# One transformer layer on one core: the first feed-forward chunk half by block products, the late modulation in 1024-wide steps, five held weight tiles at the output product's tail

## The chip, the core and the metric

The kernel runs on one core of a Trainium2 chip. A core has the matrix engine (PE, with its weight load PEld), the vector engine (DVE), the scalar engine (ACT), GpSimd (POOL) and the sync engine (SP), which here only issues DMA transfers; 16 DMA engines move the data of all queues. The metric is the device time of one execution in microseconds (us); smaller is better.

## The reference

One layer of a diffusion backbone for 128 context tokens and 512 latent tokens (640 rows, 1024 features), in float32. With SiLU(cond) through one matrix come six modulation vectors for each of the two token groups:

```python
sh1, sc1, g1, sh2, sc2, g2 = modulation(c, w_mod, b_mod)
h = rmsnorm(x, n1) * (1 + sc1) + sh1
aq, ak, av, bq, bk, bv, ga, gb = split(h @ w_in)
a_o = attention(aq, ak, av)                    # grouped-query, rotary on latents
b_o = neighbourhood_attention(bq, bk, bv)      # 8 x 16 window, learned bias
m = sigmoid(ga) * (a_o @ w_br_a) + sigmoid(gb) * (b_o @ w_br_b)
x = x + g1 * (m @ w_out)
h2 = rmsnorm(x, n2) * (1 + sc2) + sh2
x = x + g2 * (square(relu(h2 @ w_mlp_in)) @ w_mlp_out)    # 1024 -> 4096 -> 1024
y = rmsnorm(x, final_norm_g)
```

Outputs are y for both groups and the new keys and values of the context tokens.

## The kernel before

**Numbers in two parts.** Every product is done in float32 precision by splitting both operands into a high and a low part of the matrix engine's rounded type: `w_hi*x_hi + w_hi*x_lo + w_lo*x_hi`, three matmuls for each 128x128 weight block and each half of the 640 tokens (`HALVES`, 320 columns). So each weight tile that arrives by DMA is converted: ACT copies the high part, and the low part is made by DVE, by POOL, or (keys in `LOACC`) by ACT writing the negated high part and a DMA of POOL's queue adding the weights from memory onto it.

**Stages.** Features lie on partitions, tokens on columns. After the input projection and attention (which end at about 313 us) come four stages that matter here:

1. *The merge* (the loop that fills `M`, about 313 to 449 us). For each of eight feature tiles n: gate products from `w_in` tiles 18+n and 26+n (two halves each, 24 matmuls a unit, followed by `sigmoid` on ACT), then four branch products of 12 matmuls, whose PSUM results DVE multiplies with the gates (L1190), adds (L1191) and splits (ACT L1192, DVE L1193). For n = 3 and 4 both gates were computed earlier and are read back from memory by POOL's queue. `Units.ps` hands out seven PSUM banks in rotation, so unit u+7 can start once unit u has been read.
2. *The output product* (449 to 506 us). `order(KT, 4)`: the first four tiles with both halves, then the first halves of the last four, then their second halves. Four weight tiles are held for that tail: three in the ordinary pool, one in `EXTRA`. `add_gated` adds the result to x; `sq_add` accumulates the squares; `rstd_half` makes the norm of a half with two matmuls on a matrix of ones.
3. *The first feed-forward chunk* (506 to 564 us): 1024 of the 4096 hidden features, eight `w1` tiles, each a plain product with both halves. In the same stretch DVE and ACT form the second norm (`norm2`, `modulate`) and the combinations of it (`t_pieces`: T1 to T4) that later chunks need.
4. *The pairs* (564 to 922 us): `SEQ`. Layer 1 of chunks 1 to 3 and layer 2 of all chunks go by pairs of output tiles with a seven-product scheme (Strassen-Winograd): a pair takes 7 block products (A11, A12, S1 to S4, A22) of 12 matmuls where the plain way takes 8 (96 matmuls). `Operands` loads the weight tiles, adds blocks of them by accumulating DMAs of POOL's queue, and converts them ahead; six weight tiles at most are live (`W.live`).

**Late modulation.** `late_mods` computes the four modulation vectors that are needed from the output product on, as dot products on DVE. 32 tiles of 128x1024 (`wmt`, 512 KB) come by SP's queue into three buffers (tag `ms`); each takes four DVE instructions of 512 columns (L1111: two halves times two groups). A *step* is two of them. `mod_pace` spreads the 64 steps over merge and output product: every PSUM unit earns credit, and each step costs `MCOST`.

**Order.** In the merge and the output product DVE executes in the order of the program text (`MAN`); the other engines' order, and DVE's from the first chunk on, comes from the framework's scheduler. SP issues its transfers in order; a transfer whose buffer is not free holds up those behind it.

Of the kernel before, what the change touches and what calls it, by code (L numbers as in the profile page):

```python
# [16 lines left out]
P = 128  # L17
# [11 lines left out]
WP1 = 0  # L29
# [9 lines left out]
MCOST = 1500  # L39
DEFER = 60  # L40
LAG = (0, 4)
# [16 lines left out]
BLKPOOL = (("A12", "A22"), ())  # L58
# [4 lines left out]
LOTAIL = tuple(("S4", n) for n in range(4))  # L63
# [5 lines left out]
LOACC = (("in", 21, 22), ("in", 29, 30), ("in", 20, 23), ("in", 25, 26), ("in", 28, 34), ("br", 0, 8))  # L69
# [5 lines left out]
def trunk_layer(ctx: ExitStack, tc: tile.TileContext, xT, small_in, wmodA, wmodB, tabs, cacheK, cacheV, bias,  # L75
# [43 lines left out]

    def tt_tile(name):  # L120
        return cur["p"].tile([P, NT], F32R, tag="tt", bufs=12, name=name)
# [77 lines left out]
    def sq_add(acc, x, f, sl):  # L199

        q = acc if f == 0 else u("sq")
        ACT.activation(q[:, sl], x[:, sl], AF.Square)
        if 0 < f < KT - 1:
            DVE.tensor_add(acc[:, sl], acc[:, sl], q[:, sl])
        return q

    def rstd_half(acc, last, rstd, sl):
        p, n = ps_t(), sl.stop - sl.start
        PE.matmul(p[:, :n], ones, acc[:, sl], start=True, stop=False)
        PE.matmul(p[:, :n], ones, last[:, sl], start=False, stop=True)  # L210
        ACT.activation(rstd[:, sl], p[:, :n], AF.Ln, bias=eps)
        ACT.activation(rstd[:, sl], rstd[:, sl], AF.Exp, scale=-0.5)


    def w_order():
# [10 lines left out]
        for n in range(KT):  # L226
            yield ("w1", n), w1[n]
# [12 lines left out]
    class Weights:  # L240
        def __init__(self):
            self.order = list(w_order())
            self.pos = {k: i for i, (k, _) in enumerate(self.order)}
            self.st, self.t = {}, {}
            self.nd = self.nc = self.live = self.busy = 0
            self.extra = self.defer = False
# [9 lines left out]
        def conv(self):  # L256
# [4 lines left out]
            if key in EXTRA:  # L261
                self.extra = True
                hi, lo = (dp.tile([P, KT, P], F32R, tag="w4" + x, bufs=1, name="w4") for x in "hl")
# [24 lines left out]
        def done(self, *key):  # L288

            if key in EXTRA:  # L290
                self.extra = False
# [4 lines left out]
        def ahead(self):  # L296
            while self.nc < len(self.order):
                key = self.order[self.nc][0]
                if key in EXTRA and self.extra:
                    return  # L300
# [7 lines left out]
    WPOOLSET = {("out", n) for n in range(WPO, KT)} | {("w1", n) for n in range(WP1)}  # L308
    EXTRA = {("out", 4), ("w1", 0)}
# [788 lines left out]
    def late_mods():  # L1098

        cb = [tt_tile("cb") for _ in range(4)]  # L1100
        for i in range(2):
            for q in range(2):
                MISC.dma_start(r32(cb[2 * q + i][:, :512]),
                               silu[i, 4 * q:4 * q + 4].rearrange("k p -> (k p)").partition_broadcast(P))
        for n in MODS:
            st = dp.tile([P, 1024], F32, tag="ms", bufs=3, name="wmt")
            DQ[QM].dma_start(st, wmodB[n])
            for q in range(2):
                for i in range(2):
                    t = dp.tile([P, 512], F32, tag="mt", bufs=2, name="mt")  # L1110
                    DVE.scalar_tensor_tensor(t, st[:, q * 512:(q + 1) * 512], 1.0, r32(cb[2 * q + i][:, :512]), op0=OP.mult,  # L1111
                                             op1=OP.mult, accum_out=parts[:, q, n, i:i + 1])
                if q == 0:
# [122 lines left out]
    def norm_pieces(acc, last, rstd, h, apply):  # L1236
        return [lambda: None] * LAG[h] + [lambda: rstd_half(acc, last, rstd, HALVES[h])] + [lambda f=f: apply(range(f, min(f + NG, KT)))
                                                     for f in range(0, KT, NG)]

    def norm2(fs, h):  # L1240
        mod_step(16 + 4 * (fs.stop + -fs.stop % MG) - lm_n[0])
        modulate([(H2[f], X1[f], mod(2, f), mod(1, f)) for f in fs], rstd2, h)

    X1 = {}
    acc2, rstd2 = u("acc2"), u("rstd2")
    H2 = [h_pair(f"hh{f}") for f in range(KT)]
    Wt = {}
    for n, h in order(KT, 4):
        if n not in Wt:
            Wt[n] = W.get("out", n)  # L1250
            X1[n] = o_tile(f"x1_{n}")
            nc.sync.dma_start(X1[n], xT[:, n, :])
        ps = unit(Wt[n], M, h)
        if h:
            W.done("out", n)
        add_gated(n, ps, h, 0)
        sq = sq_add(acc2, X1[n], n, HALVES[h])
        if n < KT - 4 or h == 0 and n < KT - 1:
            mod_pace(OU)
        elif n == KT - 1:  # L1260
            side += norm_pieces(acc2, sq, rstd2, h, lambda fs, h=h: norm2(fs, h))

    def final(fs, sl):
        for f in fs:
            DVE.tensor_mul(X1[f][:, sl], X1[f][:, sl], rstd3[:, sl])
            (nc.sync, nc.scalar)[f % 2].dma_start(yT[:, f, sl], X1[f][:, sl])

    def relu2(dst, src, h):  # L1270

        r, sl = u("rl"), HALVES[h]
        ACT.activation(r[:, :HT], src, AF.Relu)
        if RL:
            ACT.activation(r[:, :HT], r[:, :HT], AF.Square)
            ACT.activation(dst[0][:, sl], r[:, :HT], AF.Copy)
        else:
            ACT.activation(dst[0][:, sl], r[:, :HT], AF.Square)

        def rest():  # L1280
            if not RL:
                DVE.tensor_mul(r[:, :HT], r[:, :HT], r[:, :HT])
            DVE.tensor_sub(dst[1][:, sl], r[:, :HT], r32(dst[0][:, sl]))
        flush_later(posts)
        posts.append(rest)


    T = [{}, {}, {}]
    L0, L1 = slice(0, HT), slice(HT, NT)

    def t_pieces(k):
        raw = {}

        def cut(dst, src, sl0, sl1):
            ACT.activation(dst[0][:, sl0], src, AF.Copy)
            later.append(lambda: DVE.tensor_sub(dst[1][:, sl1], src, r32(dst[0][:, sl0])))

        def p0():
            if k == 2:
                mod_step(64 - lm_n[0])  # L1300
            for i in range(3):
                T[i][k] = tt_tile(f"t{i + 1}_{k}")
            for i in range(2):
                raw[i] = u("hr")
                DVE.tensor_add(raw[i], r32(H2[k + 4 * i][0]), r32(H2[k + 4 * i][1]))
            raw[2] = u("t12")
            DVE.tensor_sub(raw[2][:, L0], raw[0][:, L1], raw[0][:, L0])
            cut((T[0][k], T[0][k]), raw[2][:, L0], L0, L1)

        def p1():  # L1310
            DVE.tensor_sub(raw[2][:, L1], raw[1][:, L1], raw[2][:, L0])
            cut((T[1][k], T[1][k]), raw[2][:, L1], L0, L1)

        def p2():
            DVE.tensor_sub(raw[0][:, L0], raw[1][:, L1], raw[0][:, L1])
            cut((T[2][k], T[2][k]), raw[0][:, L0], L0, L1)

        def p2b():
            t4[k] = tp2.get()
            DVE.tensor_sub(t4[k], raw[1][:, L0], raw[2][:, L1])  # L1320

        def p3():
            cut(H2[k], t4[k], L1, L1)
            for t in H2[k + 4]:
                ACT.activation(t[:, L1], r32(t[:, L1]), AF.Copy, scale=-1.0)

        return [p0, p1, p2, p2b, p3]
# [4 lines left out]
    def formed(i):  # L1332
# [8 lines left out]
    FIRST0 = [("A11", 0), ("A11", 1), ("A11", 2), ("A12", 0), ("A12", 1), ("A11", 3), ("A12", 2), ("A12", 3)]  # L1341
    FIRST2 = [("A11", 0), ("S1", 3, 1), ("A11", 1), ("S4", 3, 1), ("A12", 0), ("A12", 1),
              ("A11", 2), ("A11", 3), ("A12", 2), ("A12", 3)]

    def products():

        for c in range(4):
            for o, n in FIRST1 if c else ():
                yield 1, c, n, o
            for x in FIRST2 if c else FIRST0:  # L1350
# [7 lines left out]
    class Operands:  # L1358


        def __init__(self):
            self.st = {}
            self.loads = []
            for l, c, n, o in SEQ:
                k = (l, c, n, "A" if o in ("A11", "A12") else "B")
# [3 lines left out]
            self.nl = self.nc = 0  # L1369
            self.busy = {"A": 0, "B": 0}  # L1370

# [3 lines left out]
        def feed(self):  # L1375
            while self.nl < len(self.loads):
                l, c, n, x = self.loads[self.nl]
                if x == "A":
# [7 lines left out]
                nc.sync.dma_start(t, self.src(l, c, n, x == "B"))  # L1386
# [3 lines left out]
                self.busy[x] += 1  # L1390
                self.nl += 1

        def free(self, *k):
            del self.st[k]
            self.busy[k[3]] -= 1

        def conv(self):
            self.feed()
            l, c, n, o = SEQ[self.nc]
            k = (l, c, n, "A" if o in ("A11", "A12") else "B")  # L1400
            t = self.st[k]
            t = t[:, 0:4] if o in ("A11", "S3", "S2", "S4") else t[:, 4:8]
            w = wp.tile([P, KT, P], F32R, tag="w" + "hl"[self.nc % 2], bufs=3, name="wb")
            ACT.activation(w[:, 0:4], t, AF.Copy)  # L1404
            if (l, c) == (2, 3) and (o, n) in LOTAIL:
                ACT.activation(w[:, 4:8], t, AF.Copy, scale=-1.0)
                nc.gpsimd.dma_start(w[:, 4:8], t.bitcast(F32R), accum_op=OP.add)
            else:
                (nc.gpsimd if o in BLKPOOL[l - 1] else DVE).tensor_sub(w[:, 4:8], t, r32(w[:, 0:4]))  # L1409
# [10 lines left out]
        def ahead(self):  # L1420
            self.feed()
            while self.nc < len(SEQ) and W.live < 6 and (SEQ[self.nc][0], *SEQ[self.nc][1:3],
                                                         "A" if SEQ[self.nc][3] in ("A11", "A12") else "B") in self.st:
# [71 lines left out]
    def layer1(c, n, o, b, p):  # L1495
        if o == "A11":
            p.pv, p.w, p.x = tp1.get(), tp1.get(), tp2.get()
# [3 lines left out]
        if o in ("A11", "S3") and hasattr(p, "bA11") and hasattr(p, "bS3"):  # L1501
            DVE.tensor_add(p.w, p.pv, p.bS3)
            if hasattr(p, "bA22"):
                DVE.tensor_sub(p.x, p.bA22, p.w)
        if o == "S2":
# [100 lines left out]
    v_pool.close()  # L1606
    m = ctx.enter_context(tc.tile_pool(name="ops", bufs=1, side="right", reuse_waits="tile"))
# [9 lines left out]
    t4 = {}  # L1617
# [182 lines left out]
```

## Time and profile before

| | |
|---|---|
| runs | 918.33, 924.82, 922.08 us; median 922.08 |
| profiled execution | 923.55 us, span 921.8 us, clock 0.997 |
| PE busy | 901.4 us of the span, 6120 matmuls |
| DVE / ACT / POOL busy | 716.2 / 563.6 / 195.1 us |
| DMA moved | 150.04 MB, mean 163 GB/s |

The span runs from the first to the last instruction; the execution's own time is 1.75 us longer. Busy shares are means over stages with different limits, so the stages are read one by one below. Matmuls overlap in the array: one lasts about 309 ns in the trace, while the next is issued about 147 ns after it, so work on PE is counted by issues, not by durations.

### The profile page before, as it was taken

To read this page: it belongs to the slowest core of one execution; us is meant where nothing else is said; L and a number is where in the kernel's file an instruction comes from. 1 tells how busy PE (TensorE), PEld (TensorE's weight loads), DVE (VectorE), ACT (ScalarE), POOL (GpSimd) and SP (SyncE) were. 2 spreads that over 40 slices of the span, in tenths; PEclk is the share of its full clock that TensorE was granted. 3 is DMA by queue.
4 is the path that set the end of the run, shared out by engine and by line. 5 is a ranking of instruction groups with operands and counts; after the bars stand their busy time and mean duration, and the time that the engine had idled before them with its cause. 6 is when DMAs were issued, how large, how long until landed. Compare 5 with 4: busy or idle time off the path is not lost.

```text
span 921.8 us, 16618 instructions
## 1 busy us (share of the span) xinstructions
PE 901.4 (98%) x6120; PEld 871.3 (95%) x6120; DVE 716.2 (78%) x1512; ACT 563.6 (61%) x1174; POOL 195.1 (21%) x224
## 2 busy tenths in 40 slices
PE   8999999999999999899999999999999999999996
PEld 6789989989999999899999999999999999999995
DVE  6765887857666787586789995996698778985897
ACT  4566777756667765665324566536763576447775
POOL 0020200002211011111130010445234532364140
PEclk9999999999999999999999999999999999999998
DMA  9883311126535398788842362888778887898485
GB/s 345 307 242 100 89 32 41 61 67 153 155 121 136 115 278 254 202 233 247 266 154 92 105 193 92 135 189 192 171 130 193 181 174 154 163 186 190 96 124 151
DMA packets 54177, 150.04 MB, mean 163 GB/s; under 512 B 6672, under 2 KB 10400, under 8 KB 54096
## 3 DMA queue, kind: packets, MB, share of 16 engines
q1 hardware_dynamic: 31440, 99.74, 33.0%
q0 software_dynamic: 21504, 47.93, 29.9%
q10 hardware_dynamic: 1152, 1.31, 0.4%
q8 instruction: 48, 0.79, 0.4%
q14 instruction: 33, 0.27, 0.1%
HBM read 136.62 MB, written 4.60 MB: 153 GB/s over the span
## 4 chain that ended last, share of the span: by engine, by line
PE 76%; DVE 8%; DMA 6%; ACT 5%; issue 3%; POOL 1%; SPq 1%; DVEq 0%; ACTq 0%; POOLq 0%
PE b L1668 11%; PE b L1669 11%; PE b L1667 11%; PE pg L317 6%; PE pg L318 6%; PE pg L319 6%; PE pss L318 3%; PE pss L319 3%; PE pss L317 3%; PE pt L318 2%; PE pt L317 2%; PE pt L319 2%; DMA wmt<-wmodB 2%; DVE mt L1111 2%; PE pt L700 1%
## 5 line engine op out<-in xcount | busy, mean ns | idle before, releaser
L1404 ACT ACTIVATE wb<-wsb 128x512 fp32r<-128x512 f32 x140 | 87.1, 628 | 89.1 <-PE b L1669 68.6
L1668 PE MATMUL b<-op,wb 128*128 128x320 f32 x448 | 138.5, 309 | 0.3 <-DVE op L1477 0.3
L1667 PE MATMUL b<-op,wb 128*128 128x320 f32 x448 | 138.5, 309 | 0.0
L1669 PE MATMUL b<-op,wb 128*128 128x320 f32 x448 | 138.4, 309 | 0.0
L1409 DVE TENSOR_TENSOR wb<-wsb,wb 128x512 fp32r<-128x512 f32 x124 | 91.5, 742 | 26.2 <-ACT wb L1404 26.0
L1412 POOL DMA_DIRECT2D wsb<-w x84 | 73.9, 918 | 129.4 <-DVE wb L1409 104.3
L1111 DVE SCALAR_TENSOR_TENSOR mt<-wmt,cb 128x512 f32<-128x512 f32 x128 | 80.8, 687 | 7.4 <-DMA wmt<-wmodB 7.4
L1668 PEld LDWEIGHTS b<-op,wb 128*128 128x128 f32 x448 | 84.1, 188 | 0.6 <-DVE op L1477 0.6
L1667 PEld LDWEIGHTS b<-op,wb 128*128 128x128 f32 x448 | 84.1, 188 | 0.4 <-DVE x L1520 0.4
L1669 PEld LDWEIGHTS b<-op,wb 128*128 128x128 f32 x448 | 84.1, 188 | 0.0
L269 ACT ACTIVATE wh<-wst 128x512 fp32r<-128x512 f32 (+1 forms) x84 | 61.3, 740 | 34.5 <-PE pg L318 15.3
L278 DVE TENSOR_TENSOR wl<-wst,wh 128x512 fp32r<-128x512 f32 (+1 forms) x57 | 46.0, 812 | 15.8 <-ACT wh L269 13.4
L1389 POOL DMA_DIRECT2D wsb<-w x28 | 25.9, 934 | 136.7 <-DMA wsb<-w 51.9
L638 DVE TENSOR_TENSOR pl<-pt,ph 128x512 fp32r<-128x512 f32 (+1 forms) x72 | 44.9, 627 | 11.8 <-ACT ph L637 11.2
L637 ACT ACTIVATE ph<-pt 128x512 fp32r<-128x512 f32 (+1 forms) x72 | 39.3, 548 | 15.6 <-PE po L708 4.7
L1520 DVE SCALAR_TENSOR_TENSOR x<-b,parts,x 128x128 f32<-128x128 f32 (+1 forms) x116 | 46.4, 429 | 2.6 <-PE b L1669 1.9
L1404 ACT ACTIVATE wb<-wst 128x512 fp32r<-128x512 f32 x56 | 34.9, 626 | 16.7 <-PE b L1669 8.7
L1667 PE MATMUL b<-t,wb 128*128 128x320 f32 x144 | 44.6, 310 | 0.1
L1668 PE MATMUL b<-t,wb 128*128 128x320 f32 x144 | 44.5, 309 | 0.0
L1669 PE MATMUL b<-t,wb 128*128 128x320 f32 x144 | 44.5, 309 | 0.0
L1477 DVE TENSOR_TENSOR op<-hid,op 128x1280 fp32r<-128x1280 f32 (+2 forms) x32 | 37.0, 1155 | 7.4 <-ACT op L1476 7.1
L1520 DVE SCALAR_TENSOR_TENSOR x<-tp,parts,x 128x320 f32<-128x320 f32 (+2 forms) x60 | 39.2, 682 | 1.0 <-ACT tp L1571 1.0
(890 smaller groups left out, 3004.6 us busy)
## 6 DMA issues: line engine op xcount, KB each, us to landing
wsb<-w POOLq DMA_DIRECT2D x112, 256.0 KB, 5.2
wst<-w SPq DMA_DIRECT2D x36, 512.0 KB, 4.2
wmt<-wmodB SPq DMA_DIRECT2D x32, 512.0 KB, 5.7
wst<-w_in SPq DMA_DIRECT2D x31, 512.0 KB, 4.4
wsb<-w SPq DMA_DIRECT2D x28, 512.0 KB, 4.2
ms<-wmodA SPq DMA_DIRECT2D x16, 512.0 KB, 7.7
wl<-w_in POOLq DMA_DIRECT2D x8, 512.0 KB, 8.1
wst<-w_br SPq DMA_DIRECT2D x8, 512.0 KB, 5.1
```

What stands on the lines that cost most here:

```text
L269: ACT.activation(hi[:, ks], st[:, ks], AF.Copy)
L317: PE.matmul(ps, wh[:, k], xh[:, sl], start=first, stop=False)
L318: PE.matmul(ps, wh[:, k], xl[:, sl], start=False, stop=False)
L319: PE.matmul(ps, wl[:, k], xh[:, sl], start=False, stop=last)
L1111: DVE.scalar_tensor_tensor(t, st[:, q * 512:(q + 1) * 512], 1.0, r32(cb[2 * q + i][:, :512]), op0=OP.mult, op1=OP.mult, accum_out=parts[:, ...
L1404: ACT.activation(w[:, 0:4], t, AF.Copy)
L1409: (nc.gpsimd if o in BLKPOOL[l - 1] else DVE).tensor_sub(w[:, 4:8], t, r32(w[:, 0:4]))
L1412: nc.gpsimd.dma_start(t, self.src(l, c, n, e)[:, 4 * half:4 * half + 4], accum_op=OP.add)
L1520: DVE.scalar_tensor_tensor(X1[i][:, sl], src[:, sl.start - off:sl.stop - off], g[:, j:j + 1], X1[i][:, sl], op0=OP.mult, op1=OP.add)
L1667: PE.matmul(b, w[:, k], xh, start=not whole and k == 0, stop=False, skip_group_check=True)
L1668: PE.matmul(b, w[:, k], xl, start=False, stop=False, skip_group_check=True)
L1669: PE.matmul(b, w[:, 4 + k], xh, start=False, stop=o not in ("A11", "S2", "S1") and k == 3, skip_group_check=True)
```

## The change

It has these parts:

- **First chunk.** The hidden features of pairs 2 and 3 (four `w1` tiles) are computed by block products, like those of later chunks; the four tiles of pairs 0 and 1 stay whole (`C0`, `C1`: first and second half). All of it goes through `SEQ`, with up to three whole tiles interleaved in a group (first half of the k range for all, then the second half).
- **Second norm.** The normalised values are kept unsplit (`RAW0` for the first half, `RAW1` for the second); the shift is applied in place by ACT, then the split follows. T1 to T4 are made from these instead of from high + low.
- **Late modulation.** A step is one DVE instruction of 1024 columns, writing the sum straight to `mods`; `ms` has two buffers, `mt` one; `MCOST` is 1300.
- **Output product.** The tail is five tiles deep; two weight tiles are in `EXTRA`, three in the ordinary pool.
- **Smaller ones.** The low part of gate tile `("in", 31)` is made by DVE instead of by POOL's accumulating DMA; the addition in `sq_add` is deferred to the next unit; the layer-1 low parts of A12 and A22 stay on POOL for chunks 1 to 3 and are on DVE in chunk 0.

```diff
-MCOST = 1500
+MCOST = 1300
+LAG2 = 2
+TAIL = 5
-BLKPOOL = (("A12", "A22"), ())
+POOLLO = {(1, c, o) for c in (1, 2, 3) for o in ("A12", "A22")}
-LOACC = (... ("in", 28, 34), ("br", 0, 8))
+LOACC = (... ("in", 28, 31), ("in", 32, 34), ("br", 0, 8))
-    EXTRA = {("out", 4), ("w1", 0)}
+    EXTRA = {("out", n) for n in range(KT - TAIL, KT - 3)}
...
     def mods_done(n0, n1):
-        DVE.tensor_add(m, parts[:, 0, n0:n1], parts[:, 1, n0:n1])
...
-            st = dp.tile([P, 1024], F32, tag="ms", bufs=3, name="wmt")
+            st = dp.tile([P, 1024], F32, tag="ms", bufs=2, name="wmt")
             DQ[QM].dma_start(st, wmodB[n])
-            for q in range(2):
-                for i in range(2):
-                    t = dp.tile([P, 512], F32, tag="mt", bufs=2, name="mt")
-                    DVE.scalar_tensor_tensor(t, st[:, q * 512:(q + 1) * 512], 1.0, ..., accum_out=parts[:, q, n, i:i + 1])
-                if q == 0:
+            for i in range(2):
+                t = dp.tile([P, 1024], F32, tag="mt", bufs=1, name="mt")
+                DVE.scalar_tensor_tensor(t, st, 1.0, cb[i], op0=OP.mult, op1=OP.mult, accum_out=mods[:, n, i:i + 1])
+                if i == 0:
                     yield
...
-    FIRST0 = [("A11", 0), ("A11", 1), ("A11", 2), ("A12", 0), ("A12", 1), ("A11", 3), ("A12", 2), ("A12", 3)]
+    FIRST0 = [("A11", 2), ("A11", 3), ("A12", 2), ("A12", 3), ("C0", 0), ("C0", 1), ("C0", 2), ("C1", 0), ("C1", 1),
+              ("C1", 2), ("C0", 3), ("C1", 3), ("S3", 2), ("S3", 3), ("A22", 2), ("A22", 3)]
+    BEGIN2 = [("A11", 0), ("S2", 2, 1), ("S2", 3, 1), ("A11", 1), ("S1", 2, 1), ("S1", 3, 1), ("S4", 2, 1),
+              ("A12", 0), ("S4", 3, 1), ("A12", 1), ("A11", 2), ("A11", 3), ("A12", 2), ("A12", 3)]
...
+        elif n == KT - 1 and h == 0:
+            side += [rstd2_half(sq, 0)]
+            for f in range(0, KT, 2):
+                side += [lambda f=f: norm_first(f), lambda: None]
...
+    side += [lambda: None] * LAG2 + [rstd2_half(sq, 1)]
+    side += [p for f in range(0, KT, 2) for p in steps((norm_last, f))]
+    side += [p for f in (t3_piece, t2_piece, t1_piece) for k in range(4) for p in steps((f, k))]
```

More of the change, by code (lines that the diff above doesn't have):

```diff
@@ L62 @@
 SQP = 0
-LOTAIL = tuple(("S4", n) for n in range(4))
+LODMA = {(2, 3, "S4")}
+POOLLO = {(1, c, o) for c in (1, 2, 3) for o in ("A12", "A22")}
 NSUM = (1, 2)
@@ L1244, in trunk_layer @@
[L1244 to L1261, printed above, removed]
@@ L1265, in final @@
[L1265 to L1285, printed above, removed]
@@ L1504, in layer1 @@
                 DVE.tensor_sub(p.x, p.bA22, p.w)
+        if o == "A22" and not c:
+            DVE.tensor_sub(p.x, b, p.w)
         if o == "S2":
```

312 lines of the change are left out of this document (190 added, 122 removed).

## The prediction

> **What bounds the kernel now.** I read the page first, then the waits of PE, then the distances between matmuls, then DVE and SP in the stages that the change touches.
>
> ```profile
> PE 901.4 (98%) x6120; PEld 871.3 (95%) x6120; DVE 716.2 (78%) x1512; ACT 563.6 (61%) x1174; POOL 195.1 (21%) x224
> PE 76%; DVE 8%; DMA 6%; ACT 5%; issue 3%; POOL 1%; SPq 1%; DVEq 0%; ACTq 0%; POOLq 0%
> ```
>
> ```profile
> PE pg L319 <- DMA wl<-w_in: 2.2, 1, 2.2
> PE pg L317 <- DVE sg L1190: 1.2, 1, 1.2
> ```
>
> PE is busy for 98% of the span and is three quarters of the chain that ended last. The second view is the whole list of PE's waits from 330 to 620 us: two, 3.4 us together. So whatever DVE, ACT and DMA do there is hidden, save for these, and time can come from two sources only: fewer matmuls, or these waits. What a matmul costs is its distance from the next, not its duration:
>
> ```profile
> 477.95 0.31 PE L317 MATMUL pt<-mh,w 128*128 128x320 f32 x1
> 480.59 0.31 PE L317 MATMUL pss<-mh,wh 128*128 128x320 f32 x1
> 506.31 0.31 PE L317 MATMUL pss<-hh0h,w 128*128 128x320 f32 x1
> 564.17 0.31 PE L319 MATMUL pg<-hh7h,wl 128*128 128x320 f32 x1
> 516.37 0.70 PE L209 MATMUL pt<-acc,ones 128*128 128x320 f32 x2
> ```
>
> The first two rows are 18 issues apart: 2.64/18 = 0.1467 us each. The next two are the first and last matmul of the first chunk: with its last issue, 58.0 us for 8 tiles x 2 halves x 8 blocks x 3 = 384 matmuls, 56.3 us by the distance. The four matmuls on ones (last row; the next ordinary one follows at 517.44) take 1.07 us of the rest; 0.6 us is lost.
>
> How far is the cover from giving way? By stage:
>
> ```profile
> 320.00:387.00 67.00, 65.84 (x448) 65.29 (x447) 50.62 (x144) 42.47 (x84) 10.51 (x15) 1.00 0.83 243
> 387.00:454.00 67.00, 64.79 (x441) 64.34 (x440) 48.24 (x137) 37.48 (x69) 7.57 (x7) 1.00 0.84 233
> 490.00:551.00 61.00, 60.88 (x407) 59.66 (x407) 60.87 (x145) 37.94 (x79) 3.45 (x4) 1.00 0.49 139
> 551.00:580.00 29.00, 29.00 (x199) 29.00 (x199) 19.57 (x32) 20.79 (x44) 2.59 (x3) 1.00 0.30 84
> ```
>
> The columns are the length, then busy time of PE, PEld, DVE, ACT and POOL, the clock, the DMA share, GB/s. In the merge (first two rows) DMA is 83% busy and DVE 75%; from 490 to 551 us DVE has no free time at all, and still PE runs. The late modulation stands in both.
>
> **The change, part by part.**
>
> *Fewer matmuls.* The first chunk becomes 4 whole tiles x 2 x 24 = 192 plus 2 pairs x 7 x 12 = 168, so 360 in place of 384. 24 x 0.1467 = **-3.5 us** on PE's own path. Nothing hides or doubles this.
>
> *Gate tile 31.* PE's longest wait, 2.2 us, is for an accumulating transfer into `wl`, and it is the one that the change replaces by two DVE instructions of 512 columns (0.61 us each, below). **-2.2 us**, and +1.2 us of DVE in the merge.
>
> *First chunk, other engines.*
>
> ```profile
> L1111 DVE SCALAR_TENSOR_TENSOR mt<-wmt,cb 128x512 f32<-128x512 f32 x20 | 12.8, 685 | 0.0
> L278 DVE TENSOR_TENSOR wl<-wst,wh 128x1024 fp32r<-128x1024 f32 x7 | 8.6, 1222 | 0.1
> L1307 DVE TENSOR_TENSOR t<-hr 128x320 f32<-128x320 f32 x4 | 1.9, 486 | 0.0
> L1305 DVE TENSOR_TENSOR hr<-hh0h,hh0l 128x640 f32<-128x640 f32 x1 | 0.8, 817 | 0.0
> L1409 DVE TENSOR_TENSOR wb<-wst,wb 128x512 fp32r<-128x512 f32 x4 | 2.6, 687 | 2.1 <-ACT wb L1404 2.1
> L1295 ACT ACTIVATE t<-t 128x320 fp32r<-128x320 f32 x8 | 3.5, 456 | 1.4 <-DVE t L1307 1.4
> ```
>
> DVE, from 488 to 565 us: some 8 fewer late-modulation steps (-10); T1 to T4 lose eight additions of 640 columns (-6); weights go from 8 whole tiles to 4 and 14 half-size blocks (8 x 1.2 to 4 x 1.2 + 14 x 0.69, +5); pair arithmetic 2 x 5 x 0.47 (+5): -6 us, so DVE gets looser. ACT gains 16 copies of 0.46 and the blocks' high parts (7 + 5 us on 38 of 61): still below full. The orders: let the chunk start at 0. A11 and A12 of two pairs take 7.0 us; they need the first half of the norm, of tiles 4 to 7 only at 3.5, and with a tail of five units (17.6 us) it is spread over four of them and ends near 0. Before, PE met it with its 0.6 us lost; I take -0.3, ends -0.6 and 0. The second half's tiles 4 to 7 are needed at 22.9 (7.0 + 10.6 of `C0` + half of `C1`); the last `norm_last` is queued on ACT behind the eviction of the second `C0` tile at 15.8 and is through by about 22. T4 can be written once `C1` of tile 3 has read the same half (35.2) and is needed at 38.7, after S3 of both pairs; four copies and six or so negations of 0.46 on ACT end near 38. Margins of one or two us: I cost them at nothing; if ACT is late by as much again, 2 us, twice 3.5 at worst. Behind a late T4 only A22 waits, and behind that PE. The weights of the first blocks need live space, which the tail's units 5 to 7 give back at -7.0, -3.5 and 0; the first two need it by 0, with 1.3 us of conversion each. The block loads on SP and their accumulations on POOL (8 of 256 KB) fall into a stretch where DMA is 49% busy: nothing.
>
> *Late modulation.* This is where the sum is decided.
>
> ```profile
> 481.00 0.68 DVE L1111 SCALAR_TENSOR_TENSOR mt<-wmt,cb 128x512 f32<-128x512 f32 x1
> 481.61 0.68 DVE L1111 SCALAR_TENSOR_TENSOR mt<-wmt,cb 128x512 f32<-128x512 f32 x1
> 506.56 1.22 DVE L278 TENSOR_TENSOR wl<-wst,wh 128x1024 fp32r<-128x1024 f32 x1
> 507.70 0.55 DVE L1233 SCALAR_TENSOR_TENSOR x<-pg,parts,x 128x320 f32<-128x320 f32 x1
> ```
>
> A step was 2 x 0.61 = 1.22 us and becomes one instruction of 1024 columns, 1.14 us by the nearest row (its next starts 1.14 later; I count 1.15, between that and the old 1.22): 4 to 5 us of DVE saved over 64 steps. But at `MCOST` 1300 a feature tile of the merge earns 9 steps, not 8: 27 instead of 24 for n = 0 to 2, then 28 instead of 23. And `wmt` has two buffers, where three did not quite do:
>
> ```profile
> 345.17 0.69 DVE L1111 SCALAR_TENSOR_TENSOR mt<-wmt,cb 128x512 f32<-128x512 f32 x1 [0.79 <-DMA wmt<-wmodB]
> 349.97 0.69 DVE L1111 SCALAR_TENSOR_TENSOR mt<-wmt,cb 128x512 f32<-128x512 f32 x1 [2.26 <-DMA wmt<-wmodB]
> 368.03 0.69 DVE L1111 SCALAR_TENSOR_TENSOR mt<-wmt,cb 128x512 f32<-128x512 f32 x1 [3.04 <-DMA wmt<-wmodB]
> DVE mt L1111 <- DMA wmt<-wmodB: 7.4, 5, 3.0
> DMA to landing us min/median/max: 3.4/5.7/9.1
> DMA to landing us min/median/max: 5.9/7.9/8.6
> wmt<-wmodB SPq DMA_DIRECT2D x2, 512.0 KB, 4.7
> ```
>
> Behind DVE's instruction that waits stand, in text order, the gate multiplications that empty PSUM; PE may run seven units ahead and no further, and its 1.2 us wait for L1190 shows that at n = 4 it already is at that limit. Behind a `wmt` transfer that waits for its buffer stand, on SP, the weight loads of the next tiles. With two buffers a tile is asked for when the one two places before it is used up, so only one tile's 2.3 us of work covers its landing L: a wait of L - 2.3, after which the next tile comes in time. That is one wait for two tiles; branch work covers some, so I count four for n = 0 to 2 and six after.
>
> L is the unknown. The three landing rows are all `wmt` transfers, those from 322 to 345 us (six, three in flight, DMA full), and two at 438 us with nothing of POOL beside them. So 3.4 is the floor and 7.9 the far end. In the full stretch 6 tiles in 20 us came through; if two in flight get that same rate, a buffer's round is 6.7 us, 4.4 of it landing. I take 4.1, between the floor and 4.7: waits of 1.8 us.
>
> - n = 0 to 2: work 27 x 1.15 - 24 x 1.22 = +1.8; waits 4 x 1.8 - 6.1 (the three rows) = +1.1. PE is at its limit there: **+2.9 us**.
> - After that: work 28 x 1.15 - 23 x 1.22 = +4.1, tile 31 +1.2, waits 6 x 1.8 - 1.3 (7.4 less 6.1) = +9.5; together 14.8, against DVE's free time before the output product starts:
>
> ```profile
> 389.43 0.49 DVE L1190 TENSOR_TENSOR sg<-pt,sg 128x320 f32<-128x320 f32 x1 [3.61 <-ACT sg L1144]
> 427.80 0.49 DVE L1190 TENSOR_TENSOR sg<-pt,sg 128x320 f32<-128x320 f32 x1 [0.93 <-PE pt L319]
> 430.19 0.49 DVE L1193 TENSOR_TENSOR ml<-sg,mh 128x320 fp32r<-128x320 f32 x1 [1.38 <-ACT mh L1192]
> 435.78 1.23 DVE L278 TENSOR_TENSOR wl<-wst,wh 128x1024 fp32r<-128x1024 f32 x1 [3.87 <-ACT wh L269]
> 442.82 1.22 DVE L278 TENSOR_TENSOR wl<-wst,wh 128x1024 fp32r<-128x1024 f32 x1 [2.14 <-ACT wh L269]
> 450.43 1.55 DVE L1193 TENSOR_TENSOR ml<-sg,mh 128x320 fp32r<-128x320 f32 x1 [1.38 <-ACT mh L1192]
> ```
>
> The L1193 waits hold 0.54 that every merge has; the rest sums to 12.2. The overrun, **+2.6 us**, lands on the output product, whose first unit needs the last `ml`.
>
> *Smaller edits.* The fifth held tile costs no matmul. Two `cb` transfers in place of four, the additions gone from `mods_done`, the deferred sum in `sq_add`: DVE or POOL time in covered places, nothing on the path; if uncovered, below 1 us.
>
> **Sum.** -3.5 - 2.2 - 0.3 + 2.9 + 2.6 = -0.5 us on the profiled 923.55. The three runs have a median of 922.08, 1.5 below that execution, so I state 922.1 - 0.5, rounded down to **921 us**.
>
> **Rivals.**
>
> *The waits stay hidden.* At L = 3.4 the wait is 1.1: +0.1 before n = 3 and 6.6 + 4.0 < 12.2 after, so both overruns vanish and the whole -6 stands: 916; 915 if the old 1.2 us goes too. For it: each transfer meets one less in flight. Against: no `wmt` landed below 5.9 in the full stretch. The Trainium skill, "DMA: Bandwidth & Descriptors", section "Anatomy of one DMA", gives for GpSimd's path 2.0 us plus bytes over 436 GB/s: 3.2 us here, an estimate for a transfer alone. By that rule the sum is this rival's. The trace's floor of 3.4 agrees with it, its median of 5.7 does not.
>
> *Slower: two buffers throttle DVE in the merge.* At L = 5.7, the median, the wait is 3.4: 1.8 + 13.6 - 6.1 = 9.3 for n = 0 to 2, and 20.4 + 4.0 - 12.2 = 12.2 after: +15.5 net, 937. It beats the gain from L = 4.1 or 4.2 on, and passes 1% from 5.1 on (waits of 2.8). For it: DMA is 83% busy there. Against: the weight loads behind `wmt` on SP are held back with it, which thins the traffic. The same page, section "Queues, rings and completion order", says that each DMA engine takes packets from its queues in turn; the rows agree, since landings are long where POOL's transfers stand beside them.
>
> *The first chunk's operands come late* (second norm or T4, 3 to 7 us on PE): 924 to 928. For it: margins of one or two us. Against: DVE loosens by 6 us.
>
> *It does not do what it says*: the 24 matmuls replaced by as many waits or not removed; 922 to 926. The scheme is in use in later chunks, so this is small.
>
> **Chances.** A measurement of this kernel tells about 1% (9 us) from no change. Forecast, gain and throttle nearly cancelling (918 to 929, its own range): 0.43. Hidden waits (912 to 918): 0.22, of which 0.07 below 912.9. Throttle (929 and more): 0.25, nearly all past 931.3. Late operands: 0.08; not as said: 0.02. Faster by over 1% 0.07, within 0.69, slower 0.24. The range leaves out 0.07 below **913** and the throttle from L = 5.4 on (0.13) above **934**.
>
> **What would show it.** 24 matmuls fewer; no wait for `wl<-w_in`; the landing of `wmt` in the merge, and the waits of L1111 in number (about ten) and size (1.8); PE's waits for L1190 from 335 to 390 us and for `ml` at the output product's start (2.9 and 2.6); PE unbroken through the first chunk. Wrong would make it: landings near 6 us, or PE waits for T4 or `hh` tiles.

## The result, and the profile after

The changed kernel takes **945.84 us** (median of 4 runs, 944.36 to 950.1); the kernel before took 923.45 us beside it (918.33 to 924.96). The ratio is 1.0263, 95% interval 1.0230 to 1.0296: slower, and outside the predicted range. The profiled execution took 944.36 us with a span of 942.4, against 921.8 before: +20.6 us to explain.

From the page of the changed kernel, the busy shares, the chain by engine, and the group of the late modulation's steps (line L1114 now, L1111 before):

```profile
PE 906.0 (96%) x6096; PEld 873.8 (93%) x6096; DVE 715.1 (76%) x1383; ACT 571.5 (61%) x1204; POOL 201.0 (21%) x229
PE 66%; DVE 12%; DMA 9%; ACT 6%; issue 5%; POOL 1%; SPq 1%; DVEq 0%; ACTq 0%; POOLq 0%
L1114 DVE SCALAR_TENSOR_TENSOR mt<-wmt,cb 128x1024 f32<-128x1024 f32 x64 | 79.2, 1237 | 31.7 <-DMA wmt<-wmodB 30.7
```

The 24 matmuls are gone (6120 to 6096), yet PE's share of the chain fell from 76% to 66% and DVE's and DMA's rose by 4 and 3 points. The reader is to see in the last row 30.7 us of waiting for `wmt`. PE's waits, the longest of the list:

```profile
PE pss L324 <- ACT mh L1194: 6.9, 1, 6.9
PE pt L324 <- DVE sg L1192: 5.1, 1, 5.1
PE pg L324 <- DVE sg L1192: 2.0, 2, 1.4
PE b L1680 <- ACT hid L1515: 1.8, 1, 1.8
PE pg L326 <- DMA wl<-w_in: 1.5, 1, 1.5
```

To see where the 20.6 us went I cut the span at the first matmul of each stage. From PE's timeline, two rows of before (the third, at 506.31, stands in the prediction) and three of after:

```profile
317.68 0.31 PE L317 MATMUL pss<-osh,wh 128*128 128x320 f32 x1
448.72 0.31 PE L317 MATMUL pss<-mh,wh 128*128 128x320 f32 x1
```

```profile
318.38 0.31 PE L324 MATMUL pss<-osh,wh 128*128 128x320 f32 x1
460.24 0.31 PE L324 MATMUL pss<-mh,wh 128*128 128x320 f32 x1
526.43 0.31 PE L1680 MATMUL b<-hh0h,wb 128*128 128x320 f32 x1
```

The merge (first `osh` to first `mh`) grew from 131.0 to 141.9 us, the output product (to the first `hh0`) from 57.6 to 66.2, and from there to the last product it takes 405.8 instead of 405.1. From the rows that is +10.8, +8.6 and +0.7; the start and the end of the span make up the rest.

One table holds the same cut for every kernel that was run. "Lost" is the time from the first chunk's first matmul to the last product less 0.1467 us for each matmul of the products (2736 with the old first chunk, 2712 with the new): in that chunk's first 20 us, and after them. The matmuls on ones count as lost, in every row alike. One profile stands for each kernel, so read differences of 2 us or less only where several rows agree.

| kernel | time, us | merge | output product | chunks | lost in 20 us | lost later |
|---|---|---|---|---|---|---|
| before | 921 to 923 | 131.0 | 57.6 | 405.1 | 1.7 | 2.0 |
| after | 945.84 | 141.9 | 66.2 | 405.8 | 4.7 | 3.2 |
| e1_tail4_ms3 | 928.89 | 133.4 | 58.6 | 408.4 | 3.1 | 7.4 |
| e2_mt2 | 940.40 | 138.4 | 69.4 | 402.4 | 1.2 | 3.3 |
| e3_mc1500 | 951.24 | 139.8 | 74.7 | 406.9 | 2.9 | 6.1 |
| e4_before_ms2 | 935.81 | 141.4 | 58.3 | 405.8 | 1.9 | 2.5 |
| g1_blocks | 932.39 | 127.7 | 69.3 | 406.1 | 3.1 | 5.1 |
| g2_wide | 923.03 | 127.8 | 57.4 | 407.8 | 4.4 | 2.0 |
| g5_wide31 | 923.84 | 127.9 | 57.4 | 408.7 | 4.4 | 2.9 |
| g4_fill | 946.45 | 143.8 | 63.8 | 409.1 | 4.7 | 6.5 |
| h1_in31 | 920.19 | 127.1 | 57.4 | 406.4 | 1.8 | 3.2 |
| h2_wide1400 | 925.45 | 131.3 | 58.3 | 404.5 | 1.8 | 1.3 |
| h4_half | 937.23 | 135.3 | 64.4 | 403.6 | 2.7 | 3.0 |

### The profile page after: what moved, and what is told of

Its sections match the earlier page's. It is cut to its first block, busy times and chain, and to the rows that moved or that the text cites. A ratio compares the mean times of both kernels' runs of the same rounds, so it can differ in the third digit from the quotient of the medians.

```text
span 942.4 us, 16494 instructions
## 1 busy us (share of the span) xinstructions
PE 906.0 (96%) x6096; PEld 873.8 (93%) x6096; DVE 715.1 (76%) x1383; ACT 571.5 (61%) x1204; POOL 201.0 (21%) x229
## 4 chain that ended last, share of the span: by engine, by line
PE 66%; DVE 12%; DMA 9%; ACT 6%; issue 5%; POOL 1%; SPq 1%; DVEq 0%; ACTq 0%; POOLq 0%
PE b L1680 12%; PE b L1681 12%; PE b L1682 12%; DMA wmt<-wmodB 5%; PE pg L324 4%; PE pg L325 4%; PE pg L326 4%; DVE mt L1114 3%; PE pt L707 1%; DMA ms<-wmodA 1%; PE b L325 1%; PE b L324 1%; PE b L326 1%; DVE pl L645 1%; DVE wl L285 1%
## 5 line engine op out<-in xcount | busy, mean ns | idle before, releaser
L1418 ACT ACTIVATE wb<-wsb 128x512 fp32r<-128x512 f32 x150 | 93.4, 628 | 93.7 <-PE b L1682 57.9
L1682 PE MATMUL b<-op,wb 128*128 128x320 f32 x448 | 138.4, 309 | 0.0
L1423 DVE TENSOR_TENSOR wb<-wsb,wb 128x512 fp32r<-128x512 f32 x134 | 99.5, 746 | 29.2 <-ACT wb L1418 29.0
L1426 POOL DMA_DIRECT2D wsb<-w x90 | 79.7, 920 | 135.0 <-DVE wb L1423 102.3
L1114 DVE SCALAR_TENSOR_TENSOR mt<-wmt,cb 128x1024 f32<-128x1024 f32 x64 | 79.2, 1237 | 31.7 <-DMA wmt<-wmodB 30.7
L276 ACT ACTIVATE wh<-wst 128x512 fp32r<-128x512 f32 (+1 forms) x76 | 52.9, 706 | 31.7 <-PE pg L325 17.3
L1384 POOL DMA_DIRECT2D wsb<-w x30 | 28.5, 949 | 128.8 <-DMA wsb<-w 38.2
L1680 PE MATMUL b<-t,wb 128*128 128x320 f32 x168 | 52.2, 311 | 0.7 <-DVE tp L1525 0.7
L1682 PE MATMUL b<-t,wb 128*128 128x320 f32 x168 | 51.9, 309 | 0.0
L1681 PE MATMUL b<-t,wb 128*128 128x320 f32 x168 | 51.9, 309 | 0.0
L1418 ACT ACTIVATE wb<-wst 128x512 fp32r<-128x512 f32 x60 | 37.5, 626 | 15.7 <-PE b L1682 10.2
L285 DVE TENSOR_TENSOR wl<-wst,wh 128x512 fp32r<-128x512 f32 (+1 forms) x51 | 37.4, 742 | 7.4 <-ACT wh L276 5.3
```

Source lines behind the costliest of these rows:

```text
L276: ACT.activation(hi[:, ks], st[:, ks], AF.Copy)
L1114: DVE.scalar_tensor_tensor(t, st, 1.0, cb[i], op0=OP.mult, op1=OP.mult, accum_out=mods[:, n, i:i + 1])
L1423: (nc.gpsimd if (l, c, o) in POOLLO else DVE).tensor_sub(w[:, 4:8], t, r32(w[:, 0:4]))
L1426: nc.gpsimd.dma_start(t, self.src(l, c, n, e)[:, 4 * half:4 * half + 4], accum_op=OP.add)
L1680: PE.matmul(b, w[:, k], xh, start=not whole and k == 0, stop=False, skip_group_check=True)
L1681: PE.matmul(b, w[:, k], xl, start=False, stop=False, skip_group_check=True)
```

## The experiments

**Theory A**: the loss is the late modulation's: two `wmt` buffers throttle DVE in the merge, PE runs into its limit of seven units, and what DVE is late by falls on the output product's start. **Theory B**: the block products, or the width of the steps, lose the time themselves. The expectations narrow the two for each run, and some name a third, C.

### e1_tail4_ms3: three buffers back

The fifth held tile took the room of the third `wmt` buffer, so both are undone, and a second scratch tile is added in the room that this frees.

```
-TAIL = 5                                  +TAIL = 4
-tag="ms", bufs=2 ... tag="mt", bufs=1     +tag="ms", bufs=3 ... tag="mt", bufs=2
```

> The changed kernel with the tail four tiles deep again (one tile in EXTRA), which frees the room for three wmt buffers and two product tiles mt; pace (MCOST 1300), 1024-wide steps and block products stay. Theory A (two buffers leave DVE waiting for wmt, PE then waits for DVE in the merge and at the output product's start): both PE waits (5.1 and 6.9 us) and the slow clock behind them go, steps are 1.15 us apart, about 20 us less: 920 to 928. Theory B (DVE's own work at nine steps a tile is what overruns): the step's 0.1 us alone helps, 4 to 8 us less: 938 to 942. Theory C (the first chunk's late operands): no change, 945.

928.89 us, ratio to before 1.0075 [1.0052, 1.0098], just above A's range: 17 us of the 24 are back. DVE's waits for `wmt` from 310 to 530 us, and PE's longest from 300 us on:

```profile
DVE mt L1114 <- DMA wmt<-wmodB: 8.5, 6, 3.5
PE pt L326 <- DMA wl<-w_br: 2.6, 1, 2.6
PE b L1680 <- ACT hid L1515: 1.7, 1, 1.7
PE b L1680 <- DVE tp L1525: 1.4, 3, 0.9
PE b L1681 <- DVE op L1491: 1.3, 3, 0.5
PE b L1680 <- ACT op L1490: 1.3, 2, 0.9
```

The waits for `mh` and most of those for `sg` are gone with the waits for `wmt`. What is left over before is of another kind: operands of the first chunk and of the pair chunks.

### e4_before_ms2: two buffers alone

```
-            st = dp.tile([P, 1024], F32, tag="ms", bufs=3, name="wmt")
+            st = dp.tile([P, 1024], F32, tag="ms", bufs=2, name="wmt")
```

> The kernel before with two wmt buffers in place of three, nothing else. Theory A: about 8 waits of 2.3 us for wmt where 5 of 1.5 were; PE waits in the merge grow by 2 to 5 us, none at the output product's start: 925 to 930. Theory B: no change, 923.

935.81 us, ratio 1.0152 [1.0122, 1.0183]. One buffer less, in the kernel before, costs 14.5 us by the medians, more than A had set for it (the same views, from 310 to 530 us):

```profile
DVE mt L1111 <- DMA wmt<-wmodB: 28.4, 11, 5.1
PE pg L317 <- DVE sg L1190: 5.2, 1, 5.2
```

DVE waits 28.4 us instead of 7.4, and PE waits behind it. The merge takes 141.4 us, as in the changed kernel. Theory A stands, from both sides: undone in after, the loss mostly goes; done alone in before, most of it comes.

### e2_mt2: the second scratch tile

Two scratch tiles of bf16 take the room of one in f32 (the scratch is never read).

```
-                t = dp.tile([P, 1024], F32, tag="mt", bufs=1, name="mt")
+                t = dp.tile([P, 1024], mybir.dt.bfloat16, tag="mt", bufs=2, name="mt")
```

> The changed kernel with two product tiles mt in bfloat16 in place of one in float32 (same room; nothing reads them, the sums stay float32), two wmt buffers as before. It takes away only what stands between two steps. Both theories: steps 1.15 us apart in place of 1.27. Theory A: most of what DVE saves in work it waits for wmt instead, 1 to 4 us less in time: 941 to 945. Theory B: 55 steps x 0.12 = 6.6 us less in the merge and the same off PE's waits, more with the clock: 936 to 940.

940.40 us, between the two ranges; ratio 1.0204 [1.0156, 1.0252], an interval that overlaps that of after. The steps' distance does fall, as two steps of one tile show, in after and then here:

```profile
347.10 1.23 DVE L1114 SCALAR_TENSOR_TENSOR mt<-wmt,cb 128x1024 f32<-128x1024 f32 x1
348.37 1.23 DVE L1114 SCALAR_TENSOR_TENSOR mt<-wmt,cb 128x1024 f32<-128x1024 f32 x1
```

```profile
344.52 1.22 DVE L1114 SCALAR_TENSOR_TENSOR mt<-wmt,cb 128x1024 bf16<-128x1024 f32 x1
345.67 1.22 DVE L1114 SCALAR_TENSOR_TENSOR mt<-wmt,cb 128x1024 bf16<-128x1024 f32 x1
DVE mt L1114 <- DMA wmt<-wmodB: 31.2, 14, 3.8
PE pss L324 <- ACT mh L1194: 7.7, 1, 7.7
```

1.27 us with one scratch tile, 1.15 with two: a step that follows another at once waits 0.12 us until that one has let go of `mt`. This is so for 25 of the 52 steps between the merge's two cuts; the others follow another instruction, or a wait, and lose nothing. So it is 3.0 us of DVE, and not 55 x 0.12 = 6.6 as theory B had it. The merge is 3.5 us shorter and the output product 3.2 longer, so that the two together are as long as in after (207.8 and 208.1 us), with waits for `wmt` as long. The 5.4 us between the medians come from elsewhere, 3.5 of them, by the two profiles, from the first chunk's first 20 us, and no run ties them to the scratch tile.

### e3_mc1500: fewer steps in the merge

```
-MCOST = 1300
+MCOST = 1500
```

> The changed kernel at the old pace, MCOST 1500 (eight steps a feature tile in the merge, some eight steps left to the output product's tail), two buffers. Theory A: merge waits fall to about 4 us, none at the output product's start, less slow clock; 10 to 15 us less, of which late steps in the tail give back 2 to 5: 932 to 940. Theory B: nine steps fewer in the merge, 11 us less work, all of both PE waits gone: 925 to 930. Theory C: no change or slower.

951.24 us, ratio 1.0316 [1.0253, 1.0379], which neither A nor B gave; "no change or slower" was C's. PE's longest wait, and DVE's modulation steps in that window (518.0 to 533.8 us):

```profile
PE b L1680 <- ACT hh6h L1285: 15.3, 1, 15.3
L1114 DVE SCALAR_TENSOR_TENSOR mt<-wmt,cb 128x1024 f32<-128x1024 f32 x9 | 11.0, 1225 | 2.5 <-DMA wmt<-wmodB 2.3
```

Nine steps that the merge had no place for run in one block ahead of the second norm, which needs their sums, and PE stands still for the first chunk's operands, which are C's subject. So the new code, which begins the first chunk with products that need the norm, can't leave steps over: `MCOST` 1300 is part of the price of the block products.

### g1_blocks: the block products without the rest

The late modulation's code, buffers and `MCOST`, and `TAIL`, are those of before; the rest is that of after.

```
-TAIL = 5; MCOST = 1300         +TAIL = 4; MCOST = 1500
-late_mods, mods_done of after  +late_mods, mods_done of before
```

> The changed kernel with the late modulation and the tail of before (512-wide steps, three wmt buffers, MCOST 1500, TAIL 4): the block products of the first chunk and gate tile 31's conversion alone. Theory A (the loss is the late modulation's, the block products do what they say): before less 3.5 and 2.2 us plus the 1.8 us wait for hid in the first chunk, 917 to 919 us. Theory B (the block products lose their gain themselves, first by the hid wait, then by operands that come late in the pair chunks, as the kernel with TAIL 4 and three buffers hints: 313.4 us from chunk 1's first matmul to the end instead of 308.2): 922 to 928 us, with PE waits for tp and op from 600 us on of 3 us or more together.

932.39 us, ratio 1.0106 [1.0072, 1.0140], above both ranges. One wait explains the height, and it is that of e3:

```profile
PE b L1685 <- ACT hh4h L1290: 11.8, 1, 11.8
L1118 DVE SCALAR_TENSOR_TENSOR mt<-wmt,cb 128x512 f32<-128x512 f32 x14 | 8.6, 684 | 0.0
```

The second row counts DVE's steps from 503.8 to 515.8 us: 14 half steps, 7 whole ones, ahead of the norm. The merge, with three buffers and 512-wide steps, takes 127.7 us. I had meant this run to price the block products alone; with `MCOST` 1500 it can't, and e1 is the nearer answer.

### g2_wide and g5_wide31: the width, and gate tile 31 on top

g2 is before with undivided 1024-wide steps, three `wmt` buffers and two scratch tiles; g5 adds `("in", 28, 31), ("in", 32, 34)` in `LOACC`.

```
-                for i in range(2):
-                    t = dp.tile([P, 512], F32, tag="mt", bufs=2, name="mt")
...
+            for i in range(2):
+                t = dp.tile([P, 1024], F32, tag="mt", bufs=2, name="mt")
...
```

> The kernel before with steps 1024 wide, three wmt buffers and two scratch tiles; nothing else of the change (MCOST 1500, four tail tiles, no block products in the first chunk). Theory A (the width is harmless; it is the third buffer and the second scratch tile that count): step distance 1.15 us, merge as before, 919 to 923 us. Theory B (the 1024-wide step itself throttles, since a transfer's buffer is held for one undivided step): 926 us or more, with DVE waits for wmt above 15 us in the merge instead of 7.4.

> The kernel before with 1024-wide steps, three wmt buffers, two scratch tiles, and gate tile 31's low part converted on DVE. Theory A: PE's 2.2 us wait for wl<-w_in goes and nothing takes its place: about 2 us below the same kernel without tile 31, 917 to 921 us. Theory B (PE waits for something else there, such as the gate multiplications): same time as without, 919 to 923 us.

923.03 us, ratio 1.0015 [0.9995, 1.0034], and 923.84 us, 1.0026 [1.0010, 1.0043]. The width is harmless. It isn't a gain either: the merge is 3.2 us shorter than before's, and the first chunk's first 20 us lose 4.4 instead of 1.7, on small waits for `wl`, `hh6` and their like. With the width, gate tile 31 brings nothing more; there PE's wait for `wl<-w_in` was only 0.3 us.

### h1_in31 and h2_wide1400

```
-LOACC = (... ("in", 28, 34), ("br", 0, 8))
+LOACC = (... ("in", 28, 31), ("in", 32, 34), ("br", 0, 8))
```

> The kernel before with gate tile 31's low part converted by DVE and not by an accumulating transfer; nothing else. Theory A (the prediction's term): PE's 2.2 us wait for wl<-w_in at 392 us goes, nothing takes its place, the output product starts 2 us earlier and the time is 919 to 920 us. Theory B (the order of the transfers moves and another tile's transfer is waited for, or the gate multiplications are): output product's start within 1 us of 448.7, 921 to 923 us.

920.19 us, ratio 0.9986 [0.9971, 1.0002]. No wait of PE is left in the merge, which takes 127.1 us; a gain of 1 us, if it is one. In its one profile the step does what the prediction said of it.

h2 is g2 with `MCOST = 1400`:

> The kernel before with 1024-wide steps, three wmt buffers, two scratch tiles and MCOST 1400 in place of 1500, so that a few more steps stand in the merge, where the wider steps freed 4 us, and fewer in the first chunk, where they were given back. Theory A (the two stages share the steps and the freed time is given back only because DVE is full from the output product on): first chunk's lost time 2 us instead of 4.4, 919 to 921 us. Theory B (the first chunk's lost time comes from ACT's norm and not from DVE): 922 to 924 us.

925.45 us, above both ranges; ratio 1.0037 [1.0017, 1.0056]. The first chunk's loss falls to 1.8 us, as A said, but the merge takes 131.3, 3.5 us more than g2's, 2.5 of it a wait for a `wl<-w_in` that is back, and 10 slow matmuls behind that wait 1.2 more. The time moves between the stages with the steps, and nothing is won. None of these beats the kernel before by what can be told.

### h4_half: the same memory in four half tiles

```
+            half = [dp.tile([P, 512], F32, tag="ms", bufs=4, name="wmt") for _ in range(2)]
+            for q in range(2):
+                DQ[QM].dma_start(half[q], wmodB[n][:, q * 512:(q + 1) * 512])
...
```

> The changed kernel with the same memory for wmt cut into four half tiles of 512 columns, each with its own 256 KB transfer, and 512-wide steps with two scratch tiles; five tail tiles and MCOST 1300 stay. Theory A (a buffer is asked for too late: only 2.3 us of work cover a landing): three halves, 3.7 us, cover a shorter landing; DVE's waits for wmt in the merge fall from 30.7 to below 12 us, the output product starts at 449 to 453, 929 to 935 us. Theory B (the transfers' rate in a full stretch is what holds DVE back, however the memory is cut): waits above 22 us, 940 to 948 us.

937.23 us, ratio 1.0156 [1.0122, 1.0191]; the profiled run, at 931.35, is the lowest of four. In it:

```profile
DVE mt L1119 <- DMA wmt<-wmodB: 16.3, 8, 3.1
PE pg L324 <- DVE sg L1198: 4.2, 1, 4.2
wmt<-wmodB SPq DMA_DIRECT2D x51, 256.0 KB, 5.1
```

Half of the waiting goes; it and the time lie between what A and B gave. Asking earlier helps, with the same bytes in memory. But a 256 KB transfer took 5.1 us to land (median, 310 to 450 us), no less than 512 KB in the changed kernel (4.9, 320 to 450), so a part of the wait is the rate in a full stretch, and B is right on that part.

### g4_fill: PE kept busy through a wait

Forty matmuls whose output is overwritten, ahead of the last feature tile of the output product's first unit:

```
+                for _ in range(fill):
+                    PE.matmul(nxt[0], w[0][:, 0], wv[:, 128:128 + HT], start=True, stop=True)
```

> The changed kernel with 40 idle matmuls (5.9 us by 0.1467) written ahead of the matmul that starts the output product's last feature tile, on a PSUM bank that the next unit overwrites: they lie in the 6.9 us for which PE waits there. Theory A (a PE that stands idle for about 5 us gets half the clock for the next 4 to 5 us): the granted clock in the 4 us after that wait is 1.0 instead of 0.51, and the 14 issues there take 0.147 instead of 0.267 us, so 943 to 945 us. Theory B (the clock falls there for another reason than PE's idleness): it stays near 0.5, 945 to 948 us.

946.45 us, ratio 1.0269 [1.0235, 1.0302]. By stretch (length, then busy time of PE, PEld, DVE, ACT, POOL, the granted clock, DMA share, GB/s), first after, then this kernel:

```profile
358.20:363.40 5.20, 0.17 (x2) 0.00 (x0) 2.92 (x7) 0.00 (x0) 0.03 (x1) 0.87 1.03 295
363.40:368.60 5.20, 5.11 (x19) 5.11 (x20) 4.06 (x10) 3.04 (x7) 0.43 (x1) 0.50 0.52 175
463.90:470.90 7.00, 0.17 (x2) 0.00 (x0) 3.51 (x7) 2.47 (x3) 2.33 (x1) 0.78 0.94 344
470.90:474.70 3.80, 3.77 (x14) 3.77 (x15) 3.22 (x6) 0.47 (x1) 0.00 (x0) 0.51 0.51 199
```

```profile
463.00:470.00 7.00, 7.00 (x50) 7.00 (x49) 3.87 (x7) 2.01 (x2) 2.40 (x1) 1.00 0.94 331
470.00:474.00 4.00, 3.89 (x25) 3.53 (x25) 2.89 (x7) 0.94 (x2) 0.00 (x0) 1.00 0.80 314
474.00:478.00 4.00, 4.00 (x30) 4.00 (x29) 2.88 (x5) 0.47 (x1) 0.00 (x0) 1.00 0.56 170
```

In after, 5.2 us follow the first long wait at half the clock, 19 matmuls where 35 would fit, and 3.8 us the second. With the second filled, the clock stays at 1.00 behind it, and the output product takes 63.8 us instead of 66.2. So idleness is the cause here, as A said, and its price in this place 2.4 us by the two profiles, 1.7 by the count of slow matmuls. In this profile the merge was longer by 1.9 us and the chunks by 3.3, and the time lies in B's range; the gain is shown for the stage, not for the kernel.

## Why the prediction was wrong

**The late modulation.** I forecast +3.3 us for merge and output product together (2.9 + 2.6 less the 2.2 of gate tile 31); they took +19.4. Here the forecast fell: its term for the waits for `wmt` was too small, and the slow clock behind PE's own waits had no term.

- *The number of waits.* I counted ten of 1.8 us, 18 us in all, taking it that branch work covers part of them. There were 14, of 2.2 us: 30.7. Between the merge's two cuts they are 13 for 26 tiles, one for each round of the two buffers on average, so I had taken off too many for branch work.

```profile
DVE mt L1114 <- DMA wmt<-wmodB: 30.7, 14, 4.4
DMA to landing us min/median/max: 3.5/4.9/8.8
```

```profile
DMA to landing us min/median/max: 3.6/6.5/9.1
```

 The rows are after's waits from 310 to 520 us and its `wmt` landings from 320 to 450 us, then before's landings in that window. They are shorter than before's, in the direction that I gave, but a median of 4.9 and not 4.1. My own working by the rate of the full stretch had given 4.4, so waits of 2.1 us, near the 2.2 measured; I went below it, towards the floor of 3.4, and that was not borne out.
- *The step.* 1.27 us, not 1.15, where a step follows a step at once: +3.0 us of DVE in the merge. I priced the width by the nearest row and overlooked that the one `mt` holds the next step back. In e2's profile merge and output product together were no shorter without it.
- *The slack* was no error. I set 12.2 us of DVE's idle time against the overrun. The merge, from the first `osh` to the first `mh`, before and after (length, then busy time of PE, PEld and DVE, as above):

```profile
317.68:448.72 131.04, 127.68 (x867) 126.75 (x865) 97.54 (x279) 80.10 (x155) 15.68 (x21) 1.00 0.82 232
318.38:460.24 141.86, 131.62 (x867) 129.11 (x865) 100.32 (x189) 78.61 (x154) 14.77 (x20) 0.98 0.75 217
```

 DVE waits for `wmt` for 7.4 us of the first and 27.8 of the second. What is left of its idle time is 26.1 us before and 13.7 after, so 12.4 us of it did take up waits and work. Waits and work grew by 20.4 + 2.8 = 23.2 us; less 12.4, that is the 10.8 by which the merge grew. With two buffers of 1024 columns it takes 138 to 144 us in five kernels, whether steps are 512 or 1024 wide, `MCOST` 1300 or 1500, the scratch one tile or two; with three it takes 127 to 133 in seven.
- *The clock*, which stands in no term: after the waits of 5.1 and 6.9 us PE's matmuls were 0.267 us apart. 19 and 14 of them at 0.12 us more make 2.3 and 1.7 us.

The waits exceed what I had by 12.7 us and the clock adds 4.0: 16.7, against 16.1 that were missing. That is an account and no proof, though its terms are each measured: the step's 3.0 and the 2.2 of gate tile 31, which did not come, would stand on top, so some 5 us of all this was hidden, and the traces do not say where. The rival "two buffers throttle DVE" had the mechanism and 0.25 of the chance; its 937 came from L = 5.7 with my count of ten, 34 us of waits where 30.7 were measured. Its sum for merge and output product, 9.3 + 12.2 - 2.2 = 19.3, meets the 19.4, in part by luck, since the slow clock has no term in it; of the 9 us that its 937 lacks, some 4 are the first chunk's gains, which it kept and which were given back. The row that spoke for it, DMA 83% busy in the merge, was the better guide than the argument that fewer transfers in flight would each be so much faster. The rule of the Trainium skill that I weighed there ("DMA: Bandwidth & Descriptors", "Anatomy of one DMA") gives an estimate of 3.2 us for a landing; the minimum of 3.5 us agrees with it, the median does not, and the rival that rests on it, 916 us, is denied.

**24 matmuls fewer, -3.5.** Right in itself: from the first chunk on there are 2712 matmuls of the products instead of 2736, which at 0.1467 us is 397.9 us instead of 401.4. But it is given back. The first chunk's first 20 us lose 1.2 to 4.7 us in the seven kernels with the new first chunk (mean 3.2) and 1.7 to 4.4 in the six without (mean 2.7); later they lose 4.9 on average against 2.3. Net -0.4 us. The term "margins of one or two us: I cost them at nothing" was the wrong one, and the -0.3 for the norm's start is lost in it too. One of the two places is plain in the trace of after, on ACT, DVE and PE:

```profile
529.80 0.31 PE L1682 MATMUL b<-hh3h,wb 128*128 128x320 f32 x1
530.47 0.55 DVE L1235 SCALAR_TENSOR_TENSOR x<-pt,parts,x 128x320 f32<-128x320 f32 x1
531.05 0.47 ACT L211 ACTIVATE sq<-x 128x320 f32<-128x320 f32 x1 [1.00 <-DVE x L1235]
531.42 0.42 ACT L1515 ACTIVATE hid<-b 128x320 f32<-128x320 f32 x1
531.90 0.41 PE L1680 MATMUL b<-hh4h,wb 128*128 128x320 f32 x1 [1.79 <-ACT hid L1515]
```

A11 of pair 2 is done at 530; its copy stands on ACT behind a square that waits for DVE's addition of the output product, and A12 waits for the copy. I had looked at the norm's and T4's margins, and not at this copy. The other place is the pair chunks: in e1 the waits for `tp` and `op` sum to 4.0 us. That they go with the new first chunk, the table shows; whether it is its block products, its norm or its low parts that delay them was not tried and stays open.

**Gate tile 31, -2.2.** In before alone the wait goes (h1), and the gain is 0.1% with an interval that just holds none. The gate tile's own wait is gone in after too, but there a wait of 1.5 us for another `wl<-w_in` stands at 438.6 us, where before's stood at 392.6; in e1, a `wl<-w_br` of 2.6. An accumulating transfer that is late is one of several, and which one PE meets depends on the rest.

**The output product's start, +2.6.** The sign was right, the size not: 6.9 us of wait and 1.7 of slow clock. It needs both parts of the change, as far as these runs show. With two buffers but `MCOST` 1500 in before's order (e4) the output product takes 58.3 us; with `MCOST` 1300 and three buffers (e1) 58.6; with both 66.2. And after with `MCOST` 1500 alone (e3) has no wait for `mh` among its longest; its 74.7 us hold the wait for the first chunk's operands.

**What is settled.** Of the 24 us of loss, 17 go with the fifth held tile, the two buffers that it leaves room for and the one scratch tile (e1), and the buffers alone are worth 14.5 (e4). The other 7 are the new first chunk's waits, and the merge and output product, which take 3.4 us more in e1 than in before. The fifth tile's own gain wasn't seen by itself: no run has it with three buffers.

## What to carry to other kernels

A buffer that makes room for something else has a price of its own: it is the distance between asking for a tile and needing it, so count the waits at the full rate (one for each round of the buffers) and take the landing from the rate of the crowded stretch; and ask what stands in program order behind the waiting instruction. Idle time of an engine covers what is added only in part, here 12.4 of 23.2 us, and the rest reached the bottleneck. When an edit takes work off the bottleneck, add up the distances between its instructions, stage by stage, in several kernels with and without the edit: here that shows in which stages the 3.5 us are given back.

## What the hardware showed that I had not expected

PE's clock halves after a wait: granted 0.50 for 5.2 us after 5.1 us of idleness, 0.51 for 3.8 us after 6.9, and after e1's wait of 2.6 us too, 0.9 us into the work. Near that length it goes either way: behind h2's wait of 2.5 us the clock was 0.50, behind e3's of 2.7 us it stayed at 1.00, and after before's of 2.2 us the matmuls stayed 0.147 us apart. A wait of PE's of 5.1 us cost 7.4 in this way. The stretches behind h2's wait and e3's:

```profile
391.90:394.70 2.80, 2.80 (x10) 2.80 (x11) 2.55 (x5) 1.74 (x5) 0.00 (x0) 0.50 0.92 168
374.40:379.20 4.80, 4.80 (x33) 4.80 (x34) 1.90 (x3) 3.62 (x8) 0.00 (x0) 1.00 1.05 296
```

The Trainium skill, "TensorE: Matmul & The Clock Gate", Part 1, gives half the clock after an idle window of some 3.4 us and full clock after as long a busy one, with windows that run free of the program. The traces agree in the halving and, within a window, in the time at half the clock after the two long waits; g4 shows that it's the idleness. They differ in that waits of 2.5 and 2.6 us, shorter than such a window, were enough. That windows run free would explain why waits of nearly one length go either way, which no run here shows.

And smaller transfers did not land sooner in the median: 256 KB with four in the buffers took 5.1 us, 512 KB with two 4.9, in the same crowded stretch.
